# A two-block network on one core: another order of expert passes, fewer modulation steps ahead of the experts, and a convolution moved wholly to VectorE

## The chip, the cores and the metric

The kernel runs on one core of a Trainium2 chip. Time is device microseconds (us) from start to end of one execution. The kernel before took 1970.04 us, the median of three runs (1969.4 to 1972.95). One further execution was recorded by the hardware profiler; that one took 1978.85 us.

## The reference, cut to what matters

256 tokens of width 1024 go through two blocks of two layers each, in float32. The first block is where the change lies: layer 0 mixes with a gated convolution of 31 taps and a stick-breaking attention, layer 1 with a linear recurrence, and each is followed by a mixture of 16 experts of which every token uses two. Every layer is modulated by six vectors (shift, scale and gate, twice) computed from a conditioning vector c. The second block has attention of three kinds and a squared-ReLU network; it is modulated in the same way.

```python
def even_mixer(h, ...):
    u = a_val * sigmoid(a_gate)                 # 512 channels
    u = causal_dwconv(u, dw_w, dw_b)            # 31 taps per channel
    u = silu(layer_norm(u, ln_g, ln_b))
    o = stick_breaking_attention(rms_norm(q), rms_norm(k), v)
    return concatenate([u, o]) @ out_w
def moe(h2, ...):                               # 16 experts, top 2
    y = (silu(xb @ w1[e]) * (xb @ w3[e])) @ w2[e]
def first_block(x, c, ...):
    for layer in range(2):
        sh1, sc1, g1, sh2, sc2, g2 = split(silu(c) @ mod_w[layer] + mod_b[layer], 6)
        h = rms_norm(x) * (1 + sc1) + sh1
        x = x + g1 * (even_mixer(h) if layer == 0 else odd_mixer(h))
        h = rms_norm(x) * (1 + sc2) + sh2
        x = x + g2 * moe(h)
```

## The kernel before

Activations stay in SBUF transposed, as 8 tiles of 128 channels by 256 tokens. A dense product is exact to float32 by three products (L342 to L344): the weight tile `raw` is split into a high part `wh` (ACT, L330) and a low part `wl` (VectorE, L323, or now and then GpSimd), and so is the activation. Weights stream from HBM over SyncE's queue into rings of buffers: 11 of 1024 columns ("long"), 9 of 2048 columns ("wide", 1 MB, for the experts) or 6 of 1024 columns ("short"). A load is issued when the buffer that it is to fill has been read.

Each engine runs its instructions in the order in which they were placed at build, where a scheduler places them roughly in program order with a simulated readiness.

**Modulation.** The vectors of both blocks are computed in 192 steps (24 groups of eight steps, 12 groups `a` for the first block and 12 groups `b` for the second). A step takes 512 KB of `mod_w` or `w_mod` and four matmuls (L404); eight steps end with two small matmuls (L415) that turn the result into columns. In "wide" buffers two steps share one 1 MB load. `fill(n)` puts the next n steps where it stands in the program, as cover for other work; `need(group)` finishes the steps up to a group that is about to be read; `settle()` ends a group that has been begun.

**Even mixer (L515 on).** Four strips of 128 channels are gated (`u`, L545); then come the values (`ev_v`, L559), per head pair the queries and keys with their norms (L575 sums squares on PE, L478 to L480 on VectorE give the reciprocal root, L578 applies it), the attention (L589 to L603), `out_half(1)` on the attention's part, and the norm of the convolution (`colsum`, L632) with `out_half(0)`. The convolution of a strip is `conv(s, eng)`: one scaled copy on ACT and 30 taps. Strip 0 runs on GpSimd, a multiply (L531) and an add (L532) for each tap; strips 1 to 3 run on VectorE (L534) with one instruction for each tap, 90 in all, and stand behind the attention in the program, from where the scheduler moves them ahead to where VectorE is free.

**Experts (L870 on).** The router ranks the experts by their number of tokens. `PASSES` groups ranks into passes of 1, 2 or 4 experts, which share the columns of the PE array, so that a pass of any width has the same count of matmul rounds. For each pass, `prep` gathers its tokens (L929 to L940), `up_` multiplies by w1 and w3 (L955, `psab`), `down` multiplies by w2 (L955, `psY`), one pass behind `up_`, and `combine` (L996) adds the result of two passes to x. There are six loads of 1 MB for each expert, 96 for a stage, in the order of use. An expert's number is read from `idi` by SyncE (L885) before its loads can be issued. After the sixth pass stands a branch (L800) that is taken only where an expert has more tokens than room.

**Stages of the profiled execution.** Even mixer to 200 us, experts of layer 0 to 490, odd mixer to 600, experts of layer 1 to 886, second block to the end.

Of the kernel before, what the change touches and what calls it, by code (L numbers as in the profile page):

```python
# [19 lines left out]
S = 256  # L20
D = 1024
NE = 16
PASSES = [[0], [1], [2, 3], [4, 5], [6, 7], [8, 9, 10, 11], [12, 13, 14, 15]]
GROUPS = [[0, 1], [2, 3], [4, 5], [6]]
CAPS = [128 // len(p) for p in PASSES for _ in p]
# [176 lines left out]
def body(tc, A, out, co, po):  # L202
# [3 lines left out]
    with ExitStack() as ctx:  # L206
# [74 lines left out]
        def tables(want):  # L281
            if table["set"] != want:
                before = table["users"] or [table["load"]] * bool(table["load"])
                ld = SC.preload_act_table_set(want).ins
                for u in before:
                    tc.add_manual_dep(ld, u, nosync, reason="table order")
                table.update(set=want, load=ld.name, users=[])
# [231 lines left out]
        def even_mixer():  # L519
# [3 lines left out]
            NP = 1  # L523
            u, cv = Act(4, name="u"), Act(4, name="cv")

            def conv(s, eng):
                SC.activation(cv(s), u(s), AF.Identity, scale=w[:, s, 30:31], bias=Pv("dw_b")[:, s:s + 1])
                for t in range(1, 31):
                    if eng is G:
                        p = K1("cp")  # L530
                        G.tensor_mul(p[:, t:], u(s, 0, S - t), w[:, s, 30 - t:31 - t].to_broadcast([128, S - t]))  # L531
                        G.tensor_add(cv(s, t), cv(s, t), p[:, t:])  # L532
                        continue
                    eng.scalar_tensor_tensor(cv(s, t), u(s, 0, S - t), w[:, s, 30 - t:31 - t], cv(s, t),  # L534
                                             op0=OP.mult, op1=OP.add)

            for s in range(4):
# [8 lines left out]
                if s < NP:  # L546
                    conv(s, G)
            vt = [U(name="vt", bufs=2) for _ in range(2)]
            ov = [ps(), ps()]
            for j in range(4):  # L550
# [9 lines left out]
                fill(1)  # L560
            for m in range(2):
                SC.copy(vt[m], ov[m])
# [3 lines left out]
            def heads(j):  # L566

                for d, base, gn in ((q, 8, "q_g"), (k, 12, "k_g")):
# [10 lines left out]
                    fill(1)  # L579

# [44 lines left out]
            for s in range(NP, 4):  # L625
                conv(s, V)
# [26 lines left out]
        def out_proj(src, ch, cl, l):  # L653
            need(("a", l, 2))
            for n in range(8):
                o = ps()
                linear(src[n], ch, cl, o[:, :S])
                V.scalar_tensor_tensor(xT[:, n, :], o[:, :S], m1(l, 2)[:, n:n + 1], xT[:, n, :], op0=OP.mult, op1=OP.add)

# [197 lines left out]
        def moe(l):  # L857
# [20 lines left out]
            fill(20 if l == 0 else 20)  # L878
# [734 lines left out]
```

## Time and profile before

| | us |
|---|---|
| median of three runs | 1970.04 |
| profiled execution | 1978.85 |
| its span in the trace | 1976.2 |
| PE busy in the span | 1766.8 (89%) |
| VectorE busy | 1090.8 (55%) |
| ScalarE busy | 739.5 (37%) |
| GpSimd busy | 123.2 (6%) |
| transfers on SyncE's queue | 438.44 MB |

The span is the part that the trace covers; 2.65 us lie around it. PE is TensorE's matmul, PEld its weight load, DVE is VectorE, ACT is ScalarE, POOL is GpSimd, SP is SyncE. The busy shares are means over stages that differ: the second block keeps PE busy nearly throughout, the expert stages are fed from HBM, and the even mixer has stretches where VectorE is busy throughout. Matmuls on float32 operands in the expert stages appear as two records each.

### The profile page before, as it was taken

To read this page: it belongs to the slowest core of one execution; us is meant where nothing else is said; L and a number is where in the kernel's file an instruction comes from. 1 tells how busy PE (TensorE), PEld (TensorE's weight loads), DVE (VectorE), ACT (ScalarE), POOL (GpSimd) and SP (SyncE) were. 2 spreads that over 40 slices of the span, in tenths; PEclk is the share of its full clock that TensorE was granted. 3 is DMA by queue.
4 is the path that set the end of the run, shared out by engine and by line. 5 is a ranking of instruction groups with operands and counts; after the bars stand their busy time and mean duration, and the time that the engine had idled before them with its cause. 6 is when DMAs were issued, how large, how long until landed. Compare 5 with 4: busy or idle time off the path is not lost. (4 is left out here: it accounts for less than half of the span.)

```text
span 1976.2 us, 29103 instructions
## 1 busy us (share of the span) xinstructions
PE 1766.8 (89%) x11198; PEld 1262.8 (64%) x11198; DVE 1090.8 (55%) x2268; ACT 739.5 (37%) x1461; POOL 123.2 (6%) x148
## 2 busy tenths in 40 slices
PE   6699899757888997679999999999999999989997
PEld 4577544312775443127665779888888786669996
DVE  4986411102675121029777467578855767666665
ACT  3345301000563010004667346232323556544443
POOL 0900000000110000001010001000000200010000
PEclk8899999889899998898999999999999999989999
DMA  9555999997838999995101366456544230145551
GB/s 378 183 213 203 378 370 377 427 426 324 315 110 361 370 378 426 425 387 195 45 29 33 125 217 204 158 175 190 190 139 139 91 97 23 62 153 188 184 182 43
DMA packets 94233, 440.45 MB, mean 223 GB/s; under 512 B 10112, under 2 KB 10240, under 8 KB 69248
## 3 DMA queue, kind: packets, MB, share of 16 engines
q1 hardware_dynamic: 94080, 438.44, 59.4%
q8 instruction: 92, 1.51, 0.3%
q14 instruction: 61, 0.50, 0.1%
HBM read 437.35 MB, written 1.05 MB: 222 GB/s over the span
## 5 line engine op out<-in xcount | busy, mean ns | idle before, releaser
L330 ACT CAST wh<-raw 128x1024 fp32r<-128x1024 f32 (+1 forms) x258 | 261.1, 1015 | 290.2 <-PE psL L344 208.6
L323 DVE TENSOR_TENSOR wl<-raw,wh 128x1024 fp32r<-128x1024 f32 (+1 forms) x258 | 309.8, 1203 | 105.7 <-ACT wh L330 105.5
L955 PE MATMUL psab<-raw,xg 128*32 128x512 f32 (+2 forms) x1024 | 226.4, 712 | 66.0 <-DMA raw<-w 52.4
L342 PE MATMUL psL<-h,wh 128*128 128x256 f32 (+1 forms) x800 | 258.2, 323 | 7.6 <-ACT h L338 7.6
L343 PE MATMUL psL<-h,wl 128*128 128x256 f32 (+1 forms) x800 | 257.5, 322 | 3.9 <-DVE wl L323 3.8
L344 PE MATMUL psL<-h,wh 128*128 128x256 f32 (+1 forms) x800 | 256.7, 321 | 0.0
L955 PEld LDWEIGHTS psab<-raw,xg 128*32 128x32 f32 (+2 forms) x1024 | 75.2, 148 | 208.9 <-issue 187.8
L342 PE MATMUL psL<-gh,wh 128*128 128x256 f32 (+1 forms) x576 | 185.0, 322 | 0.0
L343 PE MATMUL psL<-gh,wl 128*128 128x256 f32 (+1 forms) x576 | 184.6, 321 | 0.0
L342 PEld LDWEIGHTS psL<-h,wh 128*128 128x128 f32 x800 | 154.2, 193 | 22.8 <-ACT h L338 8.3
L343 PEld LDWEIGHTS psL<-h,wl 128*128 128x128 f32 x800 | 153.9, 193 | 20.4 <-issue 6.1
L344 PEld LDWEIGHTS psL<-h,wh 128*128 128x128 f32 x800 | 153.6, 192 | 15.0 <-issue 5.4
L969 DVE SCALAR_TENSOR_TENSOR sa<-sa,gs,psab 128x512 f32<-128x512 f32 x14 | 10.5, 747 | 272.2 <-PE psab L955 272.2
L955 PE MATMUL psY<-raw,at 128*32 128x512 f32 (+2 forms) x512 | 117.6, 622 | 19.7 <-DMA raw<-w 18.0
L344 PE MATMUL psL<-o,wh 128*128 128x256 f32 (+1 forms) x384 | 119.9, 312 | 0.3
L342 PEld LDWEIGHTS psL<-gh,wh 128*128 128x128 f32 x576 | 109.5, 190 | 14.6 <-issue 5.8
L338 ACT CAST yh<-psY 128x512 fp32r<-128x512 f32 x28 | 16.4, 585 | 273.4 <-PE psY L955 273.4
L343 PEld LDWEIGHTS psL<-gh,wl 128*128 128x128 f32 x576 | 109.6, 190 | 11.1 <-issue 3.7
L955 PEld LDWEIGHTS psY<-raw,at 128*32 128x32 f32 (+2 forms) x512 | 37.2, 134 | 89.6 <-issue 65.2
L344 PE MATMUL psL<-gl,wh 128*128 128x256 f32 (+1 forms) x288 | 92.0, 319 | 0.0
L323 DVE TENSOR_TENSOR yl<-psY,yh 128x512 fp32r<-128x512 f32 x28 | 19.4, 691 | 120.5 <-ACT yh L338 120.3
L1521 ACT ACTIVATE t<-psL 128x256 f32<-128x256 f32 (+1 forms) x72 | 32.7, 455 | 139.6 <-PE psL L344 139.5
(451 smaller groups left out, 3472.3 us busy)
## 6 DMA issues: line engine op xcount, KB each, us to landing
raw<-w SPq DMA_DIRECT2D x192, 1024.0 KB, 12.0
raw<-fc SPq DMA_DIRECT2D x144, 512.0 KB, 3.6
raw<-mod_w SPq DMA_DIRECT2D x72, 512.0 KB, 7.1
raw<-w_mod SPq DMA_DIRECT2D x72, 512.0 KB, 3.9
raw<-mod_w SPq DMA_DIRECT2D x12, 1024.0 KB, 14.4
raw<-w_mod SPq DMA_DIRECT2D x12, 1024.0 KB, 14.1
raw<-wo SPq DMA_DIRECT2D x24, 512.0 KB, 4.5
raw<-wi SPq DMA_DIRECT2D x18, 512.0 KB, 3.3
```

The source lines that it names most:

```text
L323: eng.tensor_sub(o, a, hi)
L330: SC.copy(hi[:, :w], raw[:, :w])
L338: SC.copy(hi, src)
L342: T.matmul(o, lhsT=wh, rhs=xh, start=start, stop=False)
L343: T.matmul(o, lhsT=wl, rhs=xh, start=False, stop=False)
L344: T.matmul(o, lhsT=wh, rhs=xl, start=False, stop=stop)
L955: r = T.matmul(o[w * i:w * i + w, :], lhsT=x[:, w * i:w * i + w], rhs=loads[i][0][:, c:c + 512], start=first, stop=last)
L969: V.scalar_tensor_tensor(sa, sa, gs, ob, op0=OP.mult, op1=OP.mult)
L1521: SC.activation(t[:, a:b], o[:, a:b], AF.Relu)
```

## The change

Four things change. The passes of the experts run in the order 4, 1, 2, 2, 1, 2, 4 experts rather than 1, 1, 2, 2, 2, 4, 4; the ranks in a pass are the same groups, and the room for each rank's tokens (`CAPS`) is the same. `fill(20)` ahead of the experts becomes `fill(16)`, which with the ends of groups makes 16 steps there in place of 24 (eight 1 MB loads in place of twelve); eight steps are handed out one by one in the output projection of the odd mixer. The whole convolution goes to VectorE, 120 taps, and is handed out in program order: 8 pieces behind each strip, 6 in each round of the values, 5 for each head pair, the rest behind the attention. The loads of ACT's tables (L284) are held in program order.

```diff
-PASSES = [[0], [1], [2, 3], [4, 5], [6, 7], [8, 9, 10, 11], [12, 13, 14, 15]]
+PASSES = [[8, 9, 10, 11], [0], [2, 3], [4, 5], [1], [6, 7], [12, 13, 14, 15]]
...
-                ld = SC.preload_act_table_set(want).ins
+                ld = SC.preload_act_table_set(want)
+                tc.keep_in_program_order(ld)
+                ld = ld.ins
...
-            def conv(s, eng):
-                SC.activation(cv(s), u(s), AF.Identity, scale=w[:, s, 30:31], bias=Pv("dw_b")[:, s:s + 1])
-                for t in range(1, 31):
-                    if eng is G:
-                        p = K1("cp")
-                        G.tensor_mul(p[:, t:], u(s, 0, S - t), w[:, s, 30 - t:31 - t].to_broadcast([128, S - t]))
-                        G.tensor_add(cv(s, t), cv(s, t), p[:, t:])
-                        continue
-                    eng.scalar_tensor_tensor(cv(s, t), u(s, 0, S - t), w[:, s, 30 - t:31 - t], cv(s, t),
-                                             op0=OP.mult, op1=OP.add)
...
+            def tap(s, t):
+                if t == 0:
+                    SC.activation(cv(s), u(s), AF.Identity, scale=w[:, s, 30:31], bias=Pv("dw_b")[:, s:s + 1])
+                else:
+                    V.scalar_tensor_tensor(cv(s, t), u(s, 0, S - t), w[:, s, 30 - t:31 - t], cv(s, t), op0=OP.mult, op1=OP.add)
+            def taps(n):
+                for _ in range(min(n, len(pending))):
+                    tap(*pending.pop(0))
...
                 V.tensor_mul(u(s), ov[:, :S], sg)
-                if s < NP:
-                    conv(s, G)
+                pending.extend((s, t) for t in range(31))
+                taps(8)
...
                 fill(1)
+                taps(6)
...
                     fill(1)
+                    taps(5)
...
-            for s in range(NP, 4):
-                conv(s, V)
+            taps(len(pending))
...
                 V.scalar_tensor_tensor(xT[:, n, :], o[:, :S], m1(l, 2)[:, n:n + 1], xT[:, n, :], op0=OP.mult, op1=OP.add)
+                fill(1)
...
-            fill(20 if l == 0 else 20)
+            fill(16)
```

In the even mixer, VectorE's order around the first norm of the queries and keys (`nr`, L478 before, L480 after) is this; `cv` is a tap, its last number the tokens that it covers, and `wl` the low part of a weight tile. Before:

```order
L534 SCALAR_TENSOR_TENSOR cv<-u,pv,cv 128x230
L534 SCALAR_TENSOR_TENSOR cv<-u,pv,cv 128x240
L534 SCALAR_TENSOR_TENSOR cv<-u,pv,cv 128x229
L534 SCALAR_TENSOR_TENSOR cv<-u,pv,cv 128x239
L534 SCALAR_TENSOR_TENSOR cv<-u,pv,cv 128x228
L534 SCALAR_TENSOR_TENSOR cv<-u,pv,cv 128x238
L478 SCALAR_TENSOR_TENSOR nr<-psX,nr 128x256
L534 SCALAR_TENSOR_TENSOR cv<-u,pv,cv 128x227
```

After:

```order
L325 TENSOR_TENSOR wl<-raw,wh 128x1024
L532 SCALAR_TENSOR_TENSOR cv<-u,pv,cv 128x233
L532 SCALAR_TENSOR_TENSOR cv<-u,pv,cv 128x255
L532 SCALAR_TENSOR_TENSOR cv<-u,pv,cv 128x232
L532 SCALAR_TENSOR_TENSOR cv<-u,pv,cv 128x254
L532 SCALAR_TENSOR_TENSOR cv<-u,pv,cv 128x231
L532 SCALAR_TENSOR_TENSOR cv<-u,pv,cv 128x253
L532 SCALAR_TENSOR_TENSOR cv<-u,pv,cv 128x230
L325 TENSOR_TENSOR wl<-raw,wh 128x1024
L480 SCALAR_TENSOR_TENSOR nr<-psX,nr 128x256
L532 SCALAR_TENSOR_TENSOR cv<-u,pv,cv 128x229
```

Between VectorE's first tap and this `nr` stood 46 taps, 10 `wl` and 4 `u`; now stand 59 taps, 9 `wl` and 4 `u`. Before the first `cv` of the convolution's norm come another 44 taps before, and 61 after.

On PE, at the start of the experts' passes, a width of 128 is a pass of one expert, 64 of two and 32 of four (`psab` is the up product, `psY` the down product, `psX` transposes `sa`, the activated result). Before:

```order
L955 MATMUL psab<-raw,xg 128x512 x14
L955 MATMUL psY<-raw,at 128x512 x2
L972 MATMUL psX<-cst_108,sa 128x128 x4
L955 MATMUL psY<-raw,at 128x512 x6
L955 MATMUL psab<-raw,xg 64x512 x32
L955 MATMUL psY<-raw,at 128x512 x2
L972 MATMUL psX<-cst_108,sa 128x128 x4
L955 MATMUL psY<-raw,at 128x512 x6
```

After:

```order
L959 MATMUL psab<-raw,xg 128x512 x14
L976 MATMUL psX<-cst_108,sa 128x128 x4
L959 MATMUL psY<-raw,at 32x512 x32
L959 MATMUL psab<-raw,xg 64x512 x32
L959 MATMUL psY<-raw,at 128x512 x2
L976 MATMUL psX<-cst_108,sa 128x128 x4
L959 MATMUL psY<-raw,at 128x512 x6
```

Both pieces begin in the second pass's up product; behind it comes the down product of the first pass, which had one expert and now has four.

On PE, at the end of the first output projection of the second block (`cond2r` marks modulation steps, `psX` the sums of the norm that follows, `psL` the projection's products), the order before is this:

```order
L404 MATMUL psM<-raw,cond2r 32x256 x8
L463 MATMUL psX<-xT,ones 32x256 x3
L415 MATMUL psM<-cst_108,mod_e 128x8 x2
L463 MATMUL psX<-xT,ones 32x256 x5
L342 MATMUL psL<-o,wh 128x256
L343 MATMUL psL<-o,wl 128x256
L344 MATMUL psL<-o,wh 128x256
```

After:

```order
L406 MATMUL psM<-raw,cond2r 32x256 x8
L465 MATMUL psX<-xT,ones 32x256 x3
L417 MATMUL psM<-cst_108,mod_e 128x8 x2
L465 MATMUL psX<-xT,ones 32x256 x3
L406 MATMUL psM<-raw,cond2r 32x256 x16
L465 MATMUL psX<-xT,ones 32x256 x2
L469 MATMUL psX<-cs,cst_108 128x256
L406 MATMUL psM<-raw,cond2r 32x256 x8
L465 MATMUL psX<-sq,ones 32x256 x7
L406 MATMUL psM<-raw,cond2r 32x256 x8
```

Where the projection's next products stood between the sums of the norm, modulation steps stand now: the eight steps that the second expert stage no longer takes are due here, and nine loads of 512 KB of `w_mod` stand in a row on SyncE's queue, ahead of the projection's next weights.

## Rows read from the trace of the kernel before

**Rows 1.** Busy us of PE, PEld, DVE, ACT, POOL; granted clock, DMA share, GB/s.

```profile
80.00:90.00 10.00, 4.17 (x29) 3.71 (x29) 10.00 (x12) 1.96 (x5) 9.77 (x12) 0.90 0.62 203
90.00:105.00 15.00, 4.29 (x18) 4.14 (x19) 15.00 (x26) 2.24 (x4) 11.88 (x17) 0.50 0.28 111
...
105.00:160.00 55.00, 53.22 (x461) 38.34 (x460) 40.47 (x106) 27.67 (x64) 0.00 (x0) 0.97 0.69 251
```

**Rows 2.** Waits of PE in the even mixer: total us, times, longest.

```profile
PE psX L575 <- DVE nr L478: 15.5, 1, 15.5
...
PE psL L343 <- DVE wl L323: 2.1, 2, 1.0
```

**Rows 3.** Timeline of VectorE: start us, us, instruction, how many in a row.

```profile
89.80 10.43 DVE L534 SCALAR_TENSOR_TENSOR cv<-u,pv,cv 128x234 f32<-128x234 f32 x14
100.15 0.41 DVE L478 SCALAR_TENSOR_TENSOR nr<-psX,nr 128x256 f32<-128x256 f32 x1
...
102.70 0.45 DVE L534 SCALAR_TENSOR_TENSOR cv<-u,pv,cv 128x237 f32<-128x237 f32 x1
103.08 0.47 DVE L578 SCALAR_TENSOR_TENSOR q<-q,pv,rs 128x256 f32<-128x256 f32 x1
...
139.83 2.43 DVE L534 SCALAR_TENSOR_TENSOR cv<-u,pv,cv 128x233 f32<-128x233 f32 x5
```

**Rows 4.** VectorE: durations, ns min/median/max, of taps and weight splits.

```profile
L534 DVE SCALAR_TENSOR_TENSOR cv<-u,pv,cv x49: 440/806/953, 52.0 to 102.7; 128x255 f32<-128x255 f32 x2, 128x254 f32<-128x254 f32 x2, 128x253 f32<-128x253 f32 x2, 128x252 f32<-128x252 f32 x2
...
L534 DVE SCALAR_TENSOR_TENSOR cv<-u,pv,cv x42: 445/458/481, 102.7 to 147.0; 128x237 f32<-128x237 f32 x2, 128x236 f32<-128x236 f32 x2, 128x235 f32<-128x235 f32 x2, 128x234 f32<-128x234 f32 x2
...
L323 DVE TENSOR_TENSOR wl<-raw,wh x10: 1226/1712/1750, 48.0 to 88.2; 128x1024 fp32r<-128x1024 f32 x10
```

**Rows 5.** Issues of SyncE at both expert stages, then landings in the first.

```profile
190.04 27.80 SPq L319 DMA_DIRECT2D raw<-mod_w  x12
222.65 15.10 SPq L319 DMA_DIRECT2D raw<-w  x9
...
621.87 15.33 SPq L319 DMA_DIRECT2D raw<-w  x9
...
DMA to landing us min/median/max: 4.6/12.0/18.5
```

**Rows 6.** Windows in the first expert stage, columns of Rows 1.

```profile
222.00:235.00 13.00, 10.91 (x104) 9.06 (x108) 7.08 (x39) 2.26 (x5) 0.00 (x0) 0.87 1.03 422
260.00:320.00 60.00, 60.00 (x260) 28.87 (x260) 11.53 (x26) 6.05 (x11) 0.00 (x0) 1.00 0.87 340
360.00:405.00 45.00, 32.47 (x205) 11.98 (x204) 3.81 (x9) 2.83 (x4) 0.00 (x0) 0.85 1.01 426
```

**Rows 7.** Timeline of PE in that stage, columns of Rows 3, idle time ahead in brackets.

```profile
258.76 12.26 PE L955 MATMUL psab<-raw,xg 128*128 128x512 f32 x28
...
278.26 13.95 PE L955 MATMUL psab<-raw,xg 128*64 128x512 f32 x64
...
295.70 4.03 PE L955 MATMUL psY<-raw,at 128*128 128x512 f32 x9
...
308.71 3.65 PE L955 MATMUL psab<-raw,xg 128*64 128x512 f32 x16
...
412.91 1.93 PE L955 MATMUL psab<-raw,xg 128*32 128x512 f32 x8 [7.00 <-DVEq L800]
...
480.81 5.18 PE L955 MATMUL psY<-raw,at 128*32 128x512 f32 x26 [1.38 <-DMA raw<-w]
```

**Rows 8.** Window near the end of the odd mixer, columns of Rows 1.

```profile
570.00:591.00 21.00, 21.00 (x178) 20.45 (x177) 15.81 (x26) 11.58 (x17) 0.00 (x0) 1.00 0.01 2
```

**Rows 9.** Timeline of PE: modulation steps in the odd mixer, then in the second block.

```profile
556.24 1.91 PE L404 MATMUL psM<-raw,cond1r 128*32 128x256 f32 x10 [5.57 <-DMA raw<-mod_w]
...
1133.82 1.07 PE L404 MATMUL psM<-raw,cond2r 128*32 128x256 f32 x16
```

**Rows 10.** Window at the second block's first output projection, columns of Rows 1.

```profile
1134.00:1150.00 16.00, 14.04 (x101) 8.74 (x93) 7.53 (x16) 6.74 (x14) 0.00 (x0) 1.00 0.65 232
```

More of the change, by code (lines that the diff above doesn't have):

```diff
@@ L22 @@
 NE = 16
-PASSES = [[0], [1], [2, 3], [4, 5], [6, 7], [8, 9, 10, 11], [12, 13, 14, 15]]
+PASSES = [[8, 9, 10, 11], [0], [2, 3], [4, 5], [1], [6, 7], [12, 13, 14, 15]]
 GROUPS = [[0, 1], [2, 3], [4, 5], [6]]
-CAPS = [128 // len(p) for p in PASSES for _ in p]
+CAPS = [128 // len(p) for _, p in sorted((r, p) for p in PASSES for r in p)]
 ALPHA = 4.0 ** 0.25
@@ L522, in even_mixer @@
             w = Pv("dw_w").rearrange("p (a b) -> p a b", a=4)
-            NP = 1
             u, cv = Act(4, name="u"), Act(4, name="cv")
-            def conv(s, eng):
-                SC.activation(cv(s), u(s), AF.Identity, scale=w[:, s, 30:31], bias=Pv("dw_b")[:, s:s + 1])
-                for t in range(1, 31):
-                    if eng is G:
-                        p = K1("cp")
-                        G.tensor_mul(p[:, t:], u(s, 0, S - t), w[:, s, 30 - t:31 - t].to_broadcast([128, S - t]))
-                        G.tensor_add(cv(s, t), cv(s, t), p[:, t:])
-                        continue
-                    eng.scalar_tensor_tensor(cv(s, t), u(s, 0, S - t), w[:, s, 30 - t:31 - t], cv(s, t),
-                                             op0=OP.mult, op1=OP.add)
+            pending = []
+            def tap(s, t):
[6 more added lines that the diff above has]
+                    tap(*pending.pop(0))
             for s in range(4):
```

## The prediction

> **What bounds the kernel now.** I read the busy tenths by slices first, then the waits of PE stage by stage, then the windows and timelines of the stretches where PE waits. The second block keeps PE busy nearly throughout, so there only work added to PE's path matters. The two places with room are in the first block.
>
> In the even mixer PE has one wait that outweighs all others: 15.5 us for `nr` on VectorE [rows 2]. From 90 to 105 us PE is busy for 4.29 of 15 us at a granted clock of 0.50, while VectorE is busy throughout and GpSimd for 11.88 us [rows 1]. The timeline shows what VectorE did: 14 taps in a row from 89.80, and only then, at 100.15, the `nr` that PE's sums had long been ready for [rows 3]. VectorE's queue is in order, so the taps placed ahead set the time.
>
> In the expert stages the end is set by the weights. The last `down` starts at 480.81, behind a wait for a load [rows 7]. A window with full transfers moves 422 to 426 GB/s, so 1 MB (1.0486 million bytes) takes 1.0486/0.426 = 2.46 us. But between 260 and 320 us only 340 GB/s moved, while PE was busy for the whole 60 us [rows 6]: (426 - 340)/426 x 60 = 12.1 us of transfer time were lost there, because PE was slower than the loads and the nine buffers were full. Working back from the end, the first expert load landed at 480.8 - 95 x 2.46 - 12.1 = 235. It was issued at 222.65, behind modulation loads issued from 190.04 on [rows 5].
>
> **The convolution.** Until `nr`, 46 taps become 59 and 10 `wl` become 9, but GpSimd's 60 instructions fall away. Beside GpSimd a tap lasts 0.806 us and a `wl` 1.71; behind it a tap lasts 0.458 us, and the fastest `wl` 1.23 [rows 4]. What counts is the distance of starts. Two independent instructions stand 103.08 - 102.70 = 0.38 us apart; five taps on the same strip take 2.43/5 = 0.49 each [rows 3]. So the stretch costs 59 x 0.38 to 0.49, or 22 to 29 us, and 9 x 1.15 + 4 x 0.41 = 12 us for `wl` and `u` together: 34 to 41 us in place of the 52 from 48 [rows 4] to 100.15. The first `nr` would come between 82 and 89 us. PE began to wait at 100.6 - 15.5 = 85. So 11.5 to 15.5 us of the wait go; I take 13, since most of these taps alternate between two strips.
>
> The Trainium skill has a rule against counting on this: "VectorE: DVE Perf Modes", section "The DRAIN you can't avoid", says that the next instruction does not start until the pipe is empty. By it a tap would cost its whole 0.46 us whichever strip it is on, and `nr` would come 59 x 0.08 = 5 us later than with 0.38. The 0.38 of this trace speaks against it for independent instructions.
>
> What is late next: behind `nr` stand 61 taps instead of 44. The 17 more cost 6.5 to 8.3 us on VectorE, and between 105 and 160 us VectorE is busy for 40.47 of 55 us while PE is busy for 53.22 [rows 1]. The 14.5 us that VectorE is idle can hide them, unless each delays a link of the norm and attention chains by a tap. Then up to 8 us come back. On the other side up to 2.1 us of PE's waits for `wl` [rows 2] go. I take 1 us net loss: the even mixer gives **-12**, with ends of -4 (11.5 less 8) and -18 (15.5 and 2.1).
>
> **Expert stages.** With eight modulation loads ahead, SyncE still issues the first expert load at about 222.65, since it waits for the expert's number, which comes from the router. The eight loads are through by then: twelve take 12 x 2.46 = 29.5 us of transfers, and 222 to 235, at 422 GB/s [rows 6], is five loads, of which the four that go were the first. From an idle queue a load lands after 4.6 us at best [rows 5], so 227.3 in place of 235: -7.7.
>
> The new order is worth what it saves of the 12.1 lost us. An up product takes PE 14 us for one expert as for two (28 records in 12.26 us, 64 in 13.95 [rows 7]), and a down product half of that: 21 us a pass. Loads for a pass of one take 6 x 2.46 = 15 us, of two 30, of four 59. So ones starve the transfers, above all with `prep` and `combine` beside them (295.70 + 4.03 to 308.71, 9.0 us [rows 7]), and fours starve PE. I walked the 96 loads through nine buffers: a load starts when the group nine loads back has ended and lands 2.46 us after the one before it or 4.7 after its issue; PE takes 3.6 us a group of rounds (3.65 [rows 7]), 5 behind a wait, 9.0 and 7.7 us for the two `combine` with `prep`, and 7.0 at the branch [rows 7]. The walk gives 12.6 lost us before (12.1 measured) and 10.1 after: behind the four at the front, the ones and twos still leave the nine buffers full, and now the branch stands behind a one. So -7.7 - 2.4 = **-10** in the first stage. The second is built alike (first expert load at 621.87 [rows 5]): **-10** again. The ends: -7 each if the order saves nothing, and -17 each if it saves nearly all of it.
>
> **The steps that are moved.** In the odd mixer eight steps go where PE is busy for 21.00 of 21 us and transfers are idle (2 GB/s) [rows 8], so the loads are hidden and the matmuls are not: 64 records at 1.07 us for 16 [rows 9] are 4.3 us. **+4**; ends 0 (they cover a gap in the norm that follows) and +10 (with another wait as that of 5.57 us [rows 9]).
>
> The second expert stage leaves eight steps for the second block's first output projection, in one place. PE pays the same 4.3 us. The nine loads, 512 KB or 1.23 us each, hold up the projection's weights by up to 11 us, in a window where PE is busy for 14.04 of 16 us and 232 GB/s already move [rows 10]; the products that covered the norm there now come after it. **+7**; ends +4 and +16.
>
> The order of ACT's table loads is costed at nothing: ACT's own idle time hides it, 1.3 us each where it does not.
>
> **Sum.** -12 - 10 - 10 + 4 + 7 = -21 on 1978.85 is 1957.85. The profiled execution is 8.8 us longer than the median, so by the same ratio (0.9955) 1949.
>
> **Rivals.**
> 1. Transfers run full behind the four: -17 a stage, the even mixer at -16, moved steps +9. -41: 1929. For it: a four at the front is bound by transfers. Against it: by the walk the ones and twos behind it still lose 10 us. 0.11.
> 2. The gains are mostly given back: VectorE at -4, the moved steps at +4 and +14, the experts at -9 each. -4 - 9 - 9 + 4 + 14 = -4: 1966. For it: PE is nearly full wherever the steps go. Against it: VectorE has 14.5 idle us. 0.13.
> 3. The end is slower: the clock. After the four, whose groups wait for loads, PE would work through the ones and twos at less than full clock. From 360 to 405, where fours make it wait, it was granted 0.85 [rows 6]; from 260 to 320, in ones and twos, 1.00. If it did not recover, a group would cost 4.5 rather than 3.6 us, and the walk puts the last load at 493 rather than 470, 12 us after that of before; twice, with +11 for the moved steps and -12 in the even mixer, that is +23: 1993. It decides from about 4.05 us a group. Against it: before, the clock was 1.00 as soon as PE worked without a gap. 0.07.
> 4. The change does not do what it says, because VectorE's taps simply reach `nr` no sooner (waits for `u` spread them) and the experts gain only the front: 0 - 15 + 11: 1966. 0.09.
>
> "TensorE: Matmul & The Clock Gate" of the Trainium skill, section "HAM oscillation", describes rival 3's mechanism: waits for transfers between short bursts bring the clock down each time. The 0.85 of the fours agrees; no row shows it lasting into work without gaps.
>
> **How the numbers follow.** My forecast has 0.60. With rival 1 and half of rivals 2 and 4, faster by over 0.2% (below 1966; a measurement of this kernel tells about that much from no change) gets 0.82; within 0.2% 0.10, from rivals 2 and 4; slower 0.08, from rival 3 and a little of 4. The forecast's own spread is 1936 to 1960; reaching towards rivals 1 and 2, 1930 to 1967 holds 8 in 10.
>
> **What would show it.** PE's wait for `nr` below 4 us and the first `nr` before 90 us; the taps at 0.46 us throughout; the first expert load landing some five us after its issue; over 390 GB/s in each window up to the branch; the odd mixer 4 us longer; a wait of PE for `wo` or ACT's `wh` in the second block's first output projection. It is wrong if the last expert load lands less than 6 us earlier behind the first issue, if PE's clock stays below 1 in passes two to six, or if `colsum` waits for the last taps.

## The result

The changed kernel takes 1960.14 us (median of five runs, 1955.22 to 1963.2) against 1972.1 for the kernel before (five runs in the same comparison): a ratio of 0.9941, 95% interval 0.9923 to 0.996. That is 12 us, on the forecast side and inside the range, but little more than half of the 21 us that were forecast.

The two profiled executions differ by more, 1955.22 against 1978.85, because the one of before lies 7 us above its median and the one of after 5 us below. So the stages below are compared over all kernels of this study: a part that two kernels share differs by up to 6 us between their traces in the second block (the last column but one of the table) and by up to 3 in the odd mixer (133.2 to 136.4 without the moved steps), and less than that is not told apart.

The even mixer is where the time was won. PE's wait of 15.5 us for `nr` [rows 2] is gone; these are its largest waits there now (the waits of PE from 40 to 205 us, columns of Rows 2):

```profile
PE psZ L604 <- DVE ab L602: 1.1, 2, 0.8
PE psX L465 <- DVE xg L490: 1.0, 1, 1.0
PE psL L561 <- DVE wl L325: 0.8, 1, 0.8
```

VectorE's timeline (columns of Rows 3) and the durations of its taps (columns of Rows 4) show why:

```profile
77.28 1.22 DVE L325 TENSOR_TENSOR wl<-raw,wh 128x1024 fp32r<-128x1024 f32 x1
78.42 2.75 DVE L532 SCALAR_TENSOR_TENSOR cv<-u,pv,cv 128x233 f32<-128x233 f32 x7
81.08 1.21 DVE L325 TENSOR_TENSOR wl<-raw,wh 128x1024 fp32r<-128x1024 f32 x1
83.29 0.42 DVE L480 SCALAR_TENSOR_TENSOR nr<-psX,nr 128x256 f32<-128x256 f32 x1 [0.99 <-ACT nr L479]
...
L532 DVE SCALAR_TENSOR_TENSOR cv<-u,pv,cv x120: 444/463/483, 49.5 to 148.6; 128x255 f32<-128x255 f32 x4, 128x254 f32<-128x254 f32 x4, 128x253 f32<-128x253 f32 x4, 128x252 f32<-128x252 f32 x4
```

A tap lasts 0.46 us and a weight split 1.2, where beside GpSimd they lasted 0.81 and 1.71 [rows 4]; `nr` starts at 83.29 in place of 100.15 [rows 3], and VectorE now waits for ACT there, not PE for VectorE.

In the expert stage the first load lands sooner behind its issue (4.7 us in place of 11.9), but the last one by less. SyncE's queue, then windows (columns of Rows 1), then PE (columns of Rows 3):

```profile
170.68 14.05 SPq L321 DMA_DIRECT2D raw<-mod_w  x8
202.73 33.18 SPq L321 DMA_DIRECT2D raw<-w  x17
...
220.00:240.00 20.00, 10.66 (x60) 2.42 (x56) 0.00 (x0) 0.60 (x1) 0.00 (x0) 0.74 1.01 428
260.00:280.00 20.00, 19.03 (x94) 7.52 (x92) 2.17 (x7) 1.20 (x3) 0.00 (x0) 1.00 0.98 396
360.00:380.00 20.00, 19.89 (x118) 11.42 (x117) 5.62 (x13) 2.18 (x5) 0.00 (x0) 1.00 0.77 308
400.00:420.00 20.00, 12.49 (x80) 3.62 (x84) 0.00 (x0) 2.07 (x3) 0.00 (x0) 0.67 0.78 318
...
217.00 2.35 PE L959 MATMUL psab<-raw,xg 128*32 128x512 f32 x20 [1.98 <-DMA raw<-w]
...
457.55 5.34 PE L959 MATMUL psY<-raw,at 128*32 128x512 f32 x26 [1.39 <-DMA raw<-w]
```

The places at 260 to 320 us where transfers fell to 340 GB/s [rows 6] have filled, but two others have opened, at 360 to 380 and at 400 to 420, the second around the branch. From the issue of the first expert load to the arrival of the last, behind which the last products start, the stage took 480.81 - 222.65 = 258.2 us [rows 5, 7]; it takes 457.55 - 202.73 = 254.8.

### The profile page after: what moved, and what is told of

It is laid out like the page before. It is cut to its first block, busy times and chain, and to the rows that moved or that the text cites. A ratio compares the mean times of both kernels' runs of the same rounds, so it can differ in the third digit from the quotient of the medians.

```text
span 1953.4 us, 29087 instructions
## 1 busy us (share of the span) xinstructions
PE 1758.2 (90%) x11198; PEld 1256.4 (64%) x11198; DVE 1078.6 (55%) x2298; ACT 741.2 (38%) x1461; POOL 70.7 (4%) x88
## 5 line engine op out<-in xcount | busy, mean ns | idle before, releaser
L325 DVE TENSOR_TENSOR wl<-raw,wh 128x1024 fp32r<-128x1024 f32 (+1 forms) x258 | 305.3, 1185 | 97.8 <-ACT wh L332 97.4
L959 PE MATMUL psY<-raw,at 128*32 128x512 f32 (+2 forms) x512 | 113.1, 611 | 9.3 <-DMA raw<-w 8.4
L1123 DVE SCALAR_TENSOR_TENSOR xT<-psL,mod2T,xT 128x256 f32<-128x256 f32 x80 | 38.6, 483 | 84.2 <-PE psL L346 84.0
L344 PE MATMUL psL<-hh,wh 128*128 128x256 f32 x256 | 77.8, 305 | 7.0 <-ACT hh L518 5.5
```

The costliest lines, as they stand in the source:

```text
L325: eng.tensor_sub(o, a, hi)
L344: T.matmul(o, lhsT=wh, rhs=xh, start=start, stop=False)
L959: r = T.matmul(o[w * i:w * i + w, :], lhsT=x[:, w * i:w * i + w], rhs=loads[i][0][:, c:c + 512], start=first, stop=last)
L1123: V.scalar_tensor_tensor(src2[s][:, n, :], o[:, s * S:s * S + S], mod2T[l][:, g, s, n:n + 1], src2[s][:, n, :], op0=OP.mult, op1=OP.add)
```

## The experiments

The theory, once the result was known: the convolution gave what was forecast or more; the new order of passes gave nothing; the moved steps cost about what they gave. The rivals are in each run's expectation. All kernels, by stages read from their traces (us): the start of the first `nr`; the issue of the first expert load; from there to the end of the last `down` (stage 1); from there to the first load of the second expert stage (odd mixer); that stage to its last `down` (stage 2); the rest to PE's end; and the median of the timed runs.

| kernel | nr | first load | stage 1 | odd mixer | stage 2 | rest | median |
|---|---|---|---|---|---|---|---|
| before | 100.2 | 222.7 | 263.3 | 135.9 | 263.5 | 1078.4 | 1972 |
| changed | 83.3 | 202.7 | 260.2 | 143.2 | 255.9 | 1079.0 | 1960.1 |
| e1 convolution alone | 83.2 | 208.1 | 261.0 | 135.6 | 263.8 | 1072.4 | 1960.0 |
| e2 order alone | 100.6 | 220.7 | 262.6 | 135.2 | 260.7 | 1075.4 | 1972.0 |
| e3 steps alone | 100.0 | 219.9 | 260.0 | 138.8 | 259.5 | 1081.8 | 1977.8 |
| e4 all but the order | 82.2 | 201.6 | 259.5 | 143.0 | 257.3 | 1081.9 | 1957.8 |
| e5 strip 0 to VectorE, late | 81.0 | 207.9 | 262.5 | 135.9 | 264.3 | 1076.1 | 1961.1 |
| e6 taps between strips, GpSimd kept | 101.6 | 224.1 | 263.3 | 134.1 | 261.9 | 1075.9 | 1973.6 |
| e7 all but the table edit | 83.0 | 206.4 | 260.2 | 144.0 | 258.7 | 1082.1 | 1966.3 |
| e8 order 1, 4, 1, 2, 2, 2, 4 | 82.4 | 201.8 | 249.7 | 144.3 | 249.1 | 1081.4 | 1941.3 |
| e9 that order, steps as before | 82.0 | 201.6 | 255.6 | 134.8 | 254.7 | 1075.8 | 1935.2 |
| e10 that order, no steps in the odd mixer | 82.9 | 202.3 | 250.2 | 136.4 | 255.7 | 1079.6 | 1939.8 |
| e11 order 4, 1, 1, 2, 2, 2, 4 | 82.3 | 201.7 | 253.4 | 144.3 | 250.8 | 1082.2 | 1944.6 |
| e12 convolution and table edit | 83.0 | 202.5 | 263.9 | 133.2 | 265.3 | 1072.5 | 1954.1 |

e5 and e6 were run once.

### One part of the change at a time

e1 takes the convolution's hunks of the diff alone, e2 those of `PASSES` and `CAPS`, e3 the two lines on `fill`; e4 is the changed kernel with the old list:

```diff
-PASSES = [[8, 9, 10, 11], [0], [2, 3], [4, 5], [1], [6, 7], [12, 13, 14, 15]]
+PASSES = [[0], [1], [2, 3], [4, 5], [6, 7], [8, 9, 10, 11], [12, 13, 14, 15]]
```

> The kernel before with the convolution's part of the change alone: 120 taps on VectorE, handed out between the strips; pass order, modulation steps and table loads as before. Theory A (the even mixer gave more than the forecast, since GpSimd's presence also slowed the weight splits and the taps behind the first norm): first expert load issued about 20 us earlier than the 222.65 of before, near 203, and the whole about 18 to 20 us faster, near 1953. Theory B (the forecast's term): 12 us, near 1960, first expert load issued near 211. A loss elsewhere would show as a stage behind the even mixer that is longer than before's.

Measured: 1960.0 us, ratio 0.994 (0.992 to 0.9959), that is -12.4: the forecast's term. The first load comes at 208.1, between the two theories, 12.6 us earlier than in e2 and 14.6 earlier than before.

> The kernel before with the new order of passes alone (4, 1, 2, 2, 1, 2, 4), everything else as before. Theory A (the order saves no transfer time, because behind the four at the front the ones and twos leave the nine buffers full, and the branch now stands where they are full too): the span from SyncE's first expert load to the end of the last down product is 0 to 5 us longer per stage than the 263.3 of before, the whole 0 to 10 us slower (1972 to 1982), with transfers below 330 GB/s around the branch. Theory B (the forecast's walk): 2.4 us shorter per stage, the whole 5 us faster, near 1967.

Measured: ratio 1.0 (0.9985 to 1.0014). The order alone is worth nothing that can be told from zero, in the total and in both stages (262.6 and 260.7 against 263.3 and 263.5): not the 5 us of the forecast, and of theory A's range only its end at nothing. The fall of the transfers that theory A expected is there: 335 GB/s from 380 to 400 us and 316 from 420 to 440, beside the branch.

> The kernel before with the modulation steps' part alone: 16 steps ahead of the experts in place of 24, eight in the odd mixer's output projection. Theory A: the first expert load lands 5 us after its issue in place of 12, so each expert stage is 7 us shorter; the odd mixer is 7 us longer (the profile of the whole change showed 7.3 from the end of the first expert stage to the second's first load), the second block 0 to 5 longer: 2 to 7 us faster, 1965 to 1970. Theory B (the forecast): 7.5 shorter per stage, odd mixer 4 longer, second block 7 longer: 4 us faster, near 1968. The stages tell them apart, not the total.

Measured: ratio 1.0025 (1.0014 to 1.0035), 5 us slower. Neither theory had a loss. The stages are 3 to 4 us shorter, about half of the 7 that both theories had; the odd mixer is 3.0 us longer, the second block 3.4 against before's trace and 6.6 against the mean of the kernels without the moved steps (below).

> The whole change but for the order of passes, which is that of before (1, 1, 2, 2, 2, 4, 4). Theory A (the new order costs transfer time): as fast as the changed kernel or up to 8 us faster, 1952 to 1960, with less transfer time lost in the expert stages (13 us rather than 17). Theory B (the forecast's walk): 5 us slower than the changed kernel, near 1965.

Measured: 1957.8, ratio 0.9922 (0.9903 to 0.9941); the changed kernel had 0.9941 (0.9923 to 0.996). The order is worth nothing here too, at best. Theory B is out; theory A's total came true but not its reason, since e4 lost as much transfer time (18.7 and 15.7 us in its two stages from the first landing to the last, the changed kernel 17.7 and 15.0), in another place. Its windows (columns of Rows 1) show PE full while the transfers fall:

```profile
222.00:242.00 20.00, 20.00 (x83) 11.97 (x82) 4.34 (x16) 2.49 (x5) 0.00 (x0) 1.00 0.92 369
242.00:262.00 20.00, 20.00 (x71) 7.83 (x71) 2.82 (x4) 1.77 (x3) 0.00 (x0) 1.00 0.85 305
...
282.00:302.00 20.00, 19.05 (x98) 7.45 (x98) 2.21 (x7) 1.93 (x4) 0.00 (x0) 1.00 0.73 280
```

### GpSimd, or the place of the taps

e5 moves strip 0 to VectorE in the kernel before and hands out nothing; e6 hands out the taps of strips 1 to 3 as the change does, but leaves strip 0 on GpSimd:

```diff
 e5, against before
-            NP = 1
+            NP = 0
 e6, against e1
-                pending.extend((s, t) for t in range(31))
-                taps(8)
+                if s == 0:
+                    tap(0, 0)
+                    for t in range(1, 31):
+                        p = K1("cp")
+                        G.tensor_mul(p[:, t:], u(0, 0, S - t), w[:, 0, 30 - t:31 - t].to_broadcast([128, S - t]))
+                        G.tensor_add(cv(0, t), cv(0, t), p[:, t:])
+                else:
+                    pending.extend((s, t) for t in range(31))
+                    taps(8)
```

> The kernel before, with strip 0 moved from GpSimd to VectorE behind the attention like strips 1 to 3: no GpSimd work in the convolution, no taps handed out between strips (the scheduler still moves them ahead: 49 taps and 9 weight splits stand before the first norm of queries and keys). Theory A (GpSimd's work beside VectorE is what delays the norm): taps last 0.46 us throughout, the first nr starts near 83 in place of 100, the first expert load is issued near 208. Theory B (it is the placing of taps ahead of nr): nr stays behind 93.

> The convolution's part of the change alone, but with strip 0 left on GpSimd as before; taps of strips 1 to 3 are handed out between the strips (51 taps and 7 weight splits before the first nr). Theory A (GpSimd): taps at 0.7 to 0.8 us, the first nr at 95 to 102, and the first expert load issued near 218 to 222. Theory B (placing): the first nr before 88, the first load near 208.

Both runs are theory A; only e6's first load, at 224.1, is 2 us later than it had. The taps of e5, then of e6 while GpSimd works (columns of Rows 4), and the first `nr` of each (columns of Rows 3):

```profile
L534 DVE SCALAR_TENSOR_TENSOR cv<-u,pv,cv x120: 445/462/485, 50.7 to 149.2; 128x255 f32<-128x255 f32 x4, 128x254 f32<-128x254 f32 x4, 128x253 f32<-128x253 f32 x4, 128x252 f32<-128x252 f32 x4
...
76.69 4.19 DVE L534 SCALAR_TENSOR_TENSOR cv<-u,pv,cv 128x240 f32<-128x240 f32 x11
80.96 0.42 DVE L478 SCALAR_TENSOR_TENSOR nr<-psX,nr 128x256 f32<-128x256 f32 x1
```

```profile
L530 DVE SCALAR_TENSOR_TENSOR cv<-u,pv,cv x53: 444/811/954, 51.7 to 102.5; 128x255 f32<-128x255 f32 x2, 128x254 f32<-128x254 f32 x2, 128x253 f32<-128x253 f32 x2, 128x252 f32<-128x252 f32 x2
...
81.64 9.77 DVE L530 SCALAR_TENSOR_TENSOR cv<-u,pv,cv 128x235 f32<-128x235 f32 x13
101.64 0.41 DVE L478 SCALAR_TENSOR_TENSOR nr<-psX,nr 128x256 f32<-128x256 f32 x1
```

e5 has 11 taps in a row ahead of `nr` and loses nothing by them; e6 has the new handing out and gains nothing by it. The earlier `nr` comes from the absence of GpSimd's 60 instructions, not from the taps' places. In the kernel before, the `nr` at 100.15 [rows 3] ran beside a GpSimd multiply (columns of Rows 3):

```profile
99.26 1.39 POOL L531 TENSOR_TENSOR cp<-u,pv 128x227 f32<-128x227 f32 x2
```

`nr`, one of whose inputs lies in PSUM, lasts 0.41 to 0.42 us with and without GpSimd, and so does `u`, with one in PSUM too, three of which stand beside GpSimd's work in the kernel before (0.41 to 0.42); a tap and a `wl`, with two tensor inputs in SBUF, last 1.8 and 1.4 times as long beside it. The Trainium skill, "SBUF — State Buffer", section "Who interferes with whom", says this: a VectorE instruction with two SBUF inputs contends with a GpSimd instruction that reads SBUF, one with a single SBUF input (outside the 2-port modes) does not. The runs agree.

### The edit that was costed at nothing

e7 is the changed kernel, and e1 the convolution alone, without this edit; e12 is e1 with it:

```diff
-                ld = SC.preload_act_table_set(want).ins
+                ld = SC.preload_act_table_set(want)
+                tc.keep_in_program_order(ld)
+                ld = ld.ins
```

> The whole change without the edit that holds ACT's table loads in program order. Theory A (that edit, costed at nothing in the forecast, lengthens the odd mixer, which took 143 us in both kernels with it and 139 in the one with the modulation steps alone): end of the first expert stage to the second's first load 138 to 140 us, the whole 4 us faster than the changed kernel, near 1956. Theory B (the edit is free, the 143 come from the steps beside the new convolution): 143, near 1960.

The odd mixer stays at 144.0, so the edit is not what made it long; theory A falls. But the whole is not the same, as theory B had it: 1966.3, ratio 0.9963 (0.9947 to 0.9978), against 1960.1 with the edit, and the first expert load is 3.6 us later. e9 pointed the same way: with 24 steps and the edit its first load came at 201.6, where e1 without the edit had 208.1. That left the order or the edit as the cause, and e12 was made to tell them apart.

> The convolution and the edit that holds ACT's table loads in program order, with the pass order and the 24 steps of before. Theory A (with the new convolution the edit takes a table load off the router's chain: first expert load at 201.6 in the kernel that has the edit and 24 steps, 208.1 in the one with the convolution alone): first load issued near 202, odd mixer 135, second block 1076, the whole 1953 to 1956. Theory B (the 6 us are the work of the order of passes, and the edit is free): first load near 208, the whole 1960.

Measured: 1954.1, ratio 0.9911 (0.9895 to 0.9928); first load at 202.5: theory A. ACT's timelines (columns of Rows 3) in e1 and then in e12, around the split `th` of the experts' input, which VectorE waits for between the router's steps:

```profile
198.71 0.59 ACT L338 CAST th<-psY 128x512 fp32r<-128x512 f32 x1 [0.91 <-PE psY L877]
199.31 1.28 ACT L284 ACT_TABLE_LOAD   x1
200.61 1.07 ACT L338 CAST th<-psY 128x512 fp32r<-128x512 f32 x2
```

```profile
213.66 0.37 ACT L945 CAST PT<-psX 128x256 fp32r<-128x256 f32 x1 [0.25 <-PE psX L943]
214.05 1.28 ACT L284 ACT_TABLE_LOAD   x1
```

Without the edit the scheduler puts the load between two of the four splits; with it, behind the gather. That is little of the 5.6 us between 208.1 and 202.5: the four splits take 4.5 us from the first start to the last end in e1 and 3.8 in e12, and the first starts at 197.21 in e1 and at 191.94 in e12. Most of it comes earlier, with another table load. ACT around the convolution's norm (columns of Rows 3) and windows (columns of Rows 1), in e1 and then in e12:

```profile
158.48 1.28 ACT L284 ACT_TABLE_LOAD   x1
...
162.75 0.41 ACT L477 ACTIVATE nr<-rs 128x256 f32<-128x256 f32 x1
...
166.00:170.00 4.00, 2.38 (x22) 2.29 (x20) 4.00 (x11) 3.14 (x7) 0.00 (x0) 1.00 0.01 2
170.00:174.00 4.00, 4.00 (x21) 4.00 (x22) 2.55 (x7) 3.20 (x6) 0.00 (x0) 0.57 0.81 258
...
190.00:194.00 4.00, 3.49 (x16) 1.61 (x16) 3.92 (x12) 2.78 (x8) 1.59 (x2) 0.63 1.02 413
194.00:198.00 4.00, 4.00 (x20) 1.11 (x20) 1.41 (x7) 1.30 (x3) 0.00 (x0) 0.52 1.02 414
```

```profile
158.31 0.42 ACT L479 ACTIVATE nr<-rs 128x256 f32<-128x256 f32 x1
158.74 1.28 ACT L284 ACT_TABLE_LOAD   x1
...
166.00:170.00 4.00, 3.86 (x32) 3.69 (x31) 3.98 (x12) 4.00 (x10) 0.00 (x0) 1.00 0.00 0
170.00:174.00 4.00, 3.96 (x33) 3.76 (x32) 3.95 (x9) 2.02 (x4) 0.00 (x0) 1.00 0.63 195
...
190.00:194.00 4.00, 3.71 (x29) 1.59 (x27) 3.53 (x14) 3.12 (x8) 0.00 (x0) 1.00 1.03 413
194.00:198.00 4.00, 3.28 (x41) 1.66 (x41) 3.42 (x15) 1.38 (x3) 0.00 (x0) 1.00 1.02 416
```

Without the edit, ACT's part of the convolution's norm stands behind a table load and weight splits, and starts at 162.75 in place of 158.31. PE is then busy for 2.38 of the 4 us from 166, in place of 3.86, and the granted clock falls to 0.57 in the next 4 us: for most of them TensorE runs at the lower of its two levels, 1.2 in place of 2.4 GHz. The even mixer's last product ends at 183.15 in place of 180.44, which is 2.7 of the 5.6 us. From 190 to 198 the clock is low again, and the first split is 5.3 us late; what made it fall the second time is not shown. e5 and e7, which also lack the edit, have both falls; the seven kernels with the new convolution and the edit have a clock of 1.00 until 202 us.

The size is less certain than the sign. The ratio's intervals of e1 and e12 overlap at their ends, and so do those of e7 and the changed kernel; both pairs and their first loads point the same way.

### Another order

e8 and e11 change only the list in the changed kernel; e9 and e10 change e8:

```diff
 e8
+PASSES = [[0], [8, 9, 10, 11], [1], [2, 3], [4, 5], [6, 7], [12, 13, 14, 15]]
 e11
+PASSES = [[8, 9, 10, 11], [0], [1], [2, 3], [4, 5], [6, 7], [12, 13, 14, 15]]
 e10, against e8 (in out_proj)
-                fill(1)
 e9, against e10
-            fill(16)
+            fill(20)
```

> The whole change with another order of passes: 1, 4, 1, 2, 2, 2, 4. Theory A (the order matters where a one, which starves the transfers, stands next to a four, and a stage that begins with a one starts its products some 4 us sooner than one that begins with a four): first expert load to the end of the last down product 248 to 253 us per stage in place of 256 to 260, the whole 1944 to 1950. Theory B (PE's sum of work up to the branch sets the time in any order): 256 to 260, the whole within 3 us of the changed kernel.

Measured: 1941.3, ratio 0.9851 (0.9835 to 0.9868), stages of 249.7 and 249.1: theory A, with a total 3 us below its range. The first product comes 13.3 us behind the first issue, not 4 us sooner than in the changed kernel (14.3) but 1. PE's first products of the stage and the last ones behind a load, in the kernel before (the first ones; the last are in [rows 7]), in e4, in e8 and, the first ones, in e11 (columns of Rows 3):

```profile
237.29 1.12 PE L955 MATMUL psab<-raw,xg 128*128 128x512 f32 x2
```

```profile
212.53 2.82 PE L959 MATMUL psab<-raw,xg 128*128 128x512 f32 x6
...
457.48 3.64 PE L959 MATMUL psY<-raw,at 128*32 128x512 f32 x26 [1.38 <-DMA raw<-w]
```

```profile
215.12 3.25 PE L959 MATMUL psab<-raw,xg 128*128 128x512 f32 x7
...
447.88 3.64 PE L959 MATMUL psY<-raw,at 128*32 128x512 f32 x26 [1.39 <-DMA raw<-w]
```

```profile
216.36 5.34 PE L959 MATMUL psab<-raw,xg 128*32 128x512 f32 x32 [1.42 <-DMA raw<-w]
```

480.81 - 237.29 is 243.5 us, 457.48 - 212.53 is 245, 447.88 - 215.12 is 232.8. Read in this way, from the first product to the landing of the last load, the kernels fall into classes. With the old order it is 242.9 to 244.9 in all fourteen stages of before, e1, e3 to e6 and e12, whether the first load landed 2.6 us ahead of the first product or 7.5. With the order of the change it is 238.6 to 240.5 (e2: 237.1 and 238.4), in e8 to e11 it is 232.7 to 234.6. Loads land 2.44 to 2.45 us apart where the transfers run full (the median in each kernel), and 95 x 2.446 is 232.4; counted from the first landing, e8 loses 8.7 and 8.2 us of transfer time in its two stages, the changed kernel 17.7 and 15.0.

> The whole change with the order 4, 1, 1, 2, 2, 2, 4: the first two passes of the order 1, 4, 1, 2, 2, 2, 4 are exchanged, the rest is the same. Theory A (what a four at the front costs is its later first product alone): last load 233 us behind the first expert product as in the other, the first product 4 us later, the whole about 8 us slower than 1941, near 1949. Theory B (what counts is that a four stands between the two ones): last load 237 to 241 us behind the first product as in the changed kernel, the whole 1955 to 1960.

Measured: 1944.6, ratio 0.9855 (0.9819 to 0.9892); 234.6 and 233.0 us behind the first product: theory A's 233, not theory B's. The stages are 3.7 and 1.7 us longer than in e8. So it isn't a four between the ones that helps: with both ones next to each other behind a four, the stage is nearly as short. The four at the front costs less than theory A had, 1.3 us of first product behind the issue in the first stage (14.6 and 13.3) and nothing in the second (12.7 in both), and the total is 3 us slower, not 8.

> As the whole change with the order 1, 4, 1, 2, 2, 2, 4, but without the eight steps in the odd mixer's output projection; the second expert stage then takes 24 steps ahead of its experts and the second block keeps its nine loads in a row. Theory A (those eight steps are what makes the odd mixer 7 to 8 us longer): end of the first expert stage to the second's first load 136 us in place of 144, second expert stage 2 to 5 us longer, the rest 1081, the whole near 1936. Theory B (the odd mixer is longer for another reason): 141 or more, the whole at 1941 or above.

Measured: 1939.8, ratio 0.9832 (0.9803 to 0.986). The odd mixer is 136.4: theory A, the steps in its output projection are what lengthens it by 8 us. The second stage takes back 6.7 of them (255.7 after 249.1), so the total moves by 1.4 only, where 5 were expected.

> Order 1, 4, 1, 2, 2, 2, 4 and the new convolution, but the modulation steps as before the change: 24 ahead of the experts, none in the odd mixer's output projection. Theory A (moving the steps costs more than it gives: the end of a stage follows the first expert product, not the landing of the first load, by 233 us in this order): first load issued 6 us later than the 201.8 with 16 steps, odd mixer back from 144 to 136 us, second stage 2 us longer, second block 6 us shorter: 6 us faster than the 1941 of this order with 16 steps, near 1935. Theory B (the steps that were moved away from the front are worth their price in this order, since transfers bound it): 4 us slower, near 1945.

Measured: 1935.2, ratio 0.9803 (0.9775 to 0.9832), the best of all and 6 us better than e8, as theory A had it; but not by its items. The first load is not later (the edit on the tables, above); each stage is 6 us longer than in e8, since the first product comes 16.8 and 16.3 us behind the issue, not 13.3 and 12.7, and the last products take 5.3 us, not 3.6; and the odd mixer and the rest are 9.5 and 5.6 us shorter.

## Why the prediction was right, and where not

By the runs, the 12 us are: the convolution -12.4 (e1), the table edit -5.9 (e12 after e1), the moved steps +3.7 (e4 after e12; +5 in e3, and e8 is 6 slower than e9) and the order +2.3 (the changed kernel after e4), which is no larger than the scatter of its runs. The forecast had -12, 0, -4.4 (-7.7 twice, +4 and +7) and -4.8 (-2.4 twice). So one term of four came out as forecast. That the total still lies on the forecast's side and in its range it owes in part to luck: an edit costed at nothing gave 6 us.

**The convolution: right, size and mechanism.** -12 was forecast, -12.4 measured. `nr` came at 83.3, in the forecast's 82 to 89. That the two sizes meet so closely is partly chance: `nr` came 17 us sooner, where 13 were forecast, and 5 of them were gone again by e1's first load. The pitch of independent taps held: 7 in 2.75 us, which is 2.66/7 = 0.38 us from the first to the `wl` behind them (81.08 - 78.42). So the rule of the Trainium skill that was weighed there ("VectorE: DVE Perf Modes", "The DRAIN you can't avoid") would have given too late a start for such taps. The same section also says that a next op that is not held starts earlier, which the forecast left out; the trace agrees with that. Nothing was given back by the 17 more taps behind `nr`: in the changed kernel `nr` starts 17.3 us earlier than in e2, and the last product of the attention's and the convolution's part of the output ends 17.9 us earlier (180.7 and 198.7). What e1 lacks of that, its first load being 12.6 us earlier than e2's, is the table edit's part (above). No share of the taps' new places in the gain shows (e5, e6).

**The front of the expert stages: the step that failed.** "From an idle queue a load lands after 4.6 us at best [rows 5], so 227.3 in place of 235: -7.7." The landing is as forecast: 4.7 us behind the issue (207.5 after 202.73). But the stage does not end 7.7 us sooner for it. Through ones and twos PE is the bound (20.00 of 20 us in e4's first windows above), and what PE starts late with, the transfers cannot win back: with the old order the last load lands 243 to 245 us behind the first *product*. The first product waits for router, gather and the last modulation steps, and came 14.6 us behind the first issue before (237.29 and 222.65), and 10.9 in e4. So the first stage is 3 to 4 us shorter for the four loads fewer (e3 against before, e4 against e12), the second 4 to 8, and what the loads had gained beyond that was lost again where the buffers were full: 13.8 us of transfer time lost before, 18.7 in e4 (from the first landing to the last, less 95 x 2.446).

**The order: the second step that failed.** The walk had 12.6 us of transfer time lost before and 10.1 after. By the count from the first landing to the last, 13.8 and 14.1 us are lost in the two stages of before and 13.4 and 12.8 in e2; 18.7 and 15.7 in e4 and 17.7 and 15.0 in the changed kernel. That is 0.4 to 1.3 us a stage, where 2.4 were forecast, and less than such counts scatter (13.8 to 17.5 in the first stage of the five kernels with the old order and 24 steps); what excludes the forecast's 4.8 in the total is e2's interval, which ends at 3 us faster. The transfers fall in other places. The terms of the walk also have nothing for what stands ahead of the first product. In the changed kernel PE ends the gather of the first two passes at 215.01 and then waits 1.98 us for a load (217.00, above): a pass of four takes the loads of four experts side by side, and the first product starts 14.3 us behind the issue, as the fourth load lands (216.9). In all eight stages that begin with a four it starts within 0.6 us of that landing. In e4, with two ones in front, it starts 10.9 us behind the issue without a wait for a load. The order had far more in it than the walk said, but in another form: 1, 4, 1, 2, 2, 2, 4 loses 8 to 9 us of transfer time in e8, about half of what the changed kernel loses. From 360 to 380 and from 400 to 420 us, where the changed kernel moves 308 and 318 GB/s, e8 moves 426 and 427; why the rings do not fill there was not shown.

**The moved steps.** The odd mixer: +4 forecast, 0 to +10 as ends; measured +3 in e3, +8 to +10 with the new convolution (e4 after e12, e8 after e10). The matmuls were counted at 4.3 us; PE's busy time there is 121.3 us against 113.3 in e12, at a granted clock of 0.89 against 0.91. What sets e3 apart is the clock: 0.95 there and PE busy for 117.3 us, 0.87 to 0.89 and 121.1 to 123.7 us in the five kernels with the steps and the new convolution. Why the clock differs was not found. The second block: +7 forecast; the seven kernels without the burst have 1072.4 to 1078.4 there (mean 1075.2), the seven with it 1079.0 to 1082.2 (mean 1081.1): +6. PE's timeline in the changed kernel (columns of Rows 3) shows the place, then where the products resumed in the kernel before, to be read beside [rows 9, 10]:

```profile
1107.71 1.07 PE L406 MATMUL psM<-raw,cond2r 128*32 128x256 f32 x16
...
1110.33 1.93 PE L406 MATMUL psM<-raw,cond2r 128*32 128x256 f32 x32
...
1113.80 1.07 PE L406 MATMUL psM<-raw,cond2r 128*32 128x256 f32 x16
...
1117.80 1.07 PE L406 MATMUL psM<-raw,cond2r 128*32 128x256 f32 x16 [0.37 <-DMA raw<-w_mod]
...
1120.71 0.38 PE L344 MATMUL psL<-o,wh 128*128 128x256 f32 x1 [0.15 <-ACT wh L332]
1121.97 0.39 PE L345 MATMUL psL<-o,wl 128*128 128x256 f32 x1 [0.88 <-DVE wl L325]
...
1138.39 0.39 PE L342 MATMUL psL<-o,wh 128*128 128x256 f32 x1
```

Of the four groups, 5.1 us in all, one stood there before too; the rest, 4.1 us, are the 4.3 of the forecast. The projection's products resume only at 1120.71, 13 us behind the first group, and then wait for their weights; before, they resumed at 1138.39, 4.6 us behind the group at 1133.82 [rows 9].

**The table edit: missed.** It was costed at nothing because ACT has idle time. By the medians it is worth 6 us with the new convolution, as large as any other term but one. ACT's idle time says nothing on a load that stands ahead of work that PE waits for, and the price was not the 1.3 us of a load: in e1 PE's wait was followed by a stretch at the lower clock.

**The rivals.** Rival 2 came nearer to the total (1966, measured 1960) than the forecast (1949), and moved steps did cost more than they gave, but its first reason did not hold: VectorE gave nothing back. Rival 3 is out: the clock was 0.74 from 220 to 240 us, where PE waits for the four's loads, and 1.00 from 260 to 380 in each window of 20 us in which PE was busy for 19 or more. Rival 4 is out by `nr`. Rival 1 came near to true in another kernel (e8, whose stages are 13.6 and 14.4 us shorter than before's, where it had 17), not in this one.

What the forecast had named as marks: PE's wait for `nr` gone, taps at 0.46, the landing five us behind the issue, the odd mixer longer, a wait for weights in the second block, all as said; the wait for weights is small, 0.15 us for ACT's `wh` and 0.88 for `wl`. "Over 390 GB/s in each window up to the branch" failed at 360 to 380 (308). And one of the forecast's signs of being wrong did come: the last load of the first stage lands 254.8 us behind the first issue, after 258.1, which is 3.3 us earlier, less than the 6 that it had set (in the second stage 6.1). The total does not show this; the front of the expert stages, above, is the reason.

## What to carry to other kernels

An engine that lengthens another's instructions is not a second engine for free: before moving work to GpSimd, read what VectorE's instructions last beside it and alone. In a stage fed from HBM through a ring of buffers, ask which of the two ends is late where the ring is full: here a load that landed sooner was worth only as much as the first product that it let start sooner. Mix passes that PE finishes slower than their loads arrive with passes whose loads are slower, count what stands ahead of the first product (with a four at the front, its fourth load), and try several orders, because the places where the ring fills moved with each. Cost an edit that only moves small instructions by what waits behind them, the clock included.

## What was not expected of the hardware

GpSimd's instructions cost VectorE more than they took off it here: 60 of them replaced 30 taps of 0.46 us, 14 us of VectorE's time, and lengthened 49 taps and 10 splits by 0.35 and 0.49 us each, 22 us. The other place of a table load of 1.28 us went with a stretch at the lower of TensorE's two clock levels (granted 0.57 from 170 to 174 us in e1, 1.00 in e12). And runs of one kernel scatter by 2 to 14 us here (1967.48 to 1981.27 for the kernel before in 23 runs), which is more than most terms of this study; the stages of the traces told more than the totals.
